# Modulation vectors from row-major weights on VectorE, gate rows built from columns, and an issue order searched from four first ranks

## The chip, the cores and the metric

The kernel runs on one core of one Trainium2 chip. The metric is the device time of one execution in microseconds (us); lower is better. Engines are named as in the profile: PE is TensorE (matmuls; PEld its weight loads), DVE is VectorE, ACT is ScalarE, POOL is GpSimd, SP is the queue that issues every DMA.

## What is computed

A two-layer transformer block with modulation, followed by a third mixer block that the change does not touch. What matters here is the modulation: a vector `c` of 1024 values gives, for each of two layers, 3072 numbers (shift, scale, gate), through a 1024 x 3072 matrix.

```python
cond = jax.nn.silu(c)
for layer in range(DEPTH):                       # DEPTH = 2, D_MODEL = 1024, SEQ = 512
    mod = cond @ w_ada[layer] + b_ada[layer]
    shift, scale, gate = jnp.split(mod, 3, axis=-1)
    h = rmsnorm(x, g_pre[layer]) * (1.0 + scale[:, None, :]) + shift[:, None, :]
    y = even_mixer(h, ...) if layer % 2 == 0 else odd_mixer(h, ...)
    x = x + gate[:, None, :] * rmsnorm(y, g_post[layer])
```

All inputs and the output are float32. The mixers are projections of `h`, several kinds of attention, a gate and an output projection.

## The kernel before

**Modulation.** `w_ada` lies in memory as in the reference: a row per input, 3072 outputs along it. One product of 1024 outputs takes eight transfers of 512 KB (128 inputs on the partitions, 1024 outputs along the row). For each, DVE multiplies the tile by the column `cond[:, k]` and adds it to an accumulator [128, 1024] (`gemv_acc`, L175 for the first, L177 for the other seven). The sum over the 128 partitions is still open then. For shift and scale, `gemv_cols` (L183) closes it with eight PE matmuls against a column of ones, one output column each, and DVE adds the bias (L185): the result is a column tile [128, 8]. For the gate, `gate_row` (L204) closes it with two PE matmuls of ones [128,128] by 512 columns, so that the result stands on all partitions as a row [128, 1024]; bias and `g_post` are broadcast from memory as rows, DVE adds (L216) and POOL multiplies (L217).

**The start.** `first_h` (L645) loads four token blocks `P` of `x`, sums their squares on ACT (L135), scales them (L671), and PE transposes them (L140) into PSUM, from where ACT copies them to `qk` (L677). The scale vector of layer 0 (`pthr` is its accumulator) gives `moda` (L685), with which ACT writes `hh` (L687) and DVE `hl` (L693). Then PE multiplies with the first three weight chunks (`whir` and `wlor` are the two halves of a loaded weight `wrawr`, written by ACT at L109 and POOL or DVE at L113; `accr` is PSUM). The shift vector of layer 0 (`sa`) is summed meanwhile and applied afterwards (L724 to L727).

**The background.** The other four products (scale and shift of layer 1, the two gates) run as background steps through one buffer, `graw`: layer 1's and gate 0 during layer 0, gate 1 during layer 1. The gate row is needed where layer 0 and layer 1 end (`residual`, L606 and following, at about 268 us and 564 us of the profile).

**The order.** What an engine issues next is set by `Plan.pin` (L2043): it reads all instructions, gives each a rank (its place in the program, mixed with the length of the path behind it, weight `PATH`), lists them by a model of durations, ranks them backward from the result, and repeats this six times; the order with the shortest modelled end is fixed for every engine. So a change anywhere moves instructions everywhere.

## Time and profile before

| | |
|---|---|
| median of 3 runs | 960.73 us (960.22 to 961.03) |
| the profiled execution's own time | 959.33 us |
| span of that execution, first to last instruction | 957.6 us |
| PE busy | 908.6 us (95%) |
| DVE busy | 707.7 us (74%) |
| ACT busy | 535.0 us (56%) |
| POOL busy | 243.7 us (25%) |

The profile is of one execution. Its own time is 1.7 us above its span (what lies before the first and behind the last instruction), and 1.4 us below the median of the runs. A busy share is a mean over the span; an engine that is busy is not always the one that the others wait for.

### The profile page before, as it was taken

How to read it: one execution, taken by the hardware profiler on the slowest of the kernel's cores; microseconds unless marked ns; L12 is line 12 of the kernel's file. 1: busy time of each engine (PE TensorE's matmuls, PEld its weight loads, DVE VectorE, ACT ScalarE, POOL GpSimd, SP SyncE). 2: the span in 40 equal slices, each digit the busy share in tenths (PEclk: the TensorE clock that was granted, in tenths of full speed). 3: DMA queues.
4: the chain of work that ended last, by engine and by line, in shares of the span. 5: the costliest groups of instructions: out<-in, count | busy, mean ns of one | idle time of the engine just before them, and what ended most of it. 6: DMA issues, size and time to landing. Idle time of an engine off the chain costs nothing.

```text
span 957.6 us, 14806 instructions
## 1 busy us (share of the span) xinstructions
PE 908.6 (95%) x5001; PEld 764.1 (80%) x5001; DVE 707.7 (74%) x1581; ACT 535.0 (56%) x1182; POOL 243.7 (25%) x274
## 2 busy tenths in 40 slices
PE   0999999889989989999999999999999999999996
PEld 0888888768868878889888878987888888888775
DVE  5876869858989747875465766377598788687857
ACT  5544677648735435584365944464444486676820
POOL 0330133113410012321021420024044335444530
PEclk9999999989999999999999999999999999999998
DMA  9747644456575555631754534234323344430152
GB/s 350 291 134 213 193 134 140 144 159 162 160 238 203 181 166 142 197 103 48 196 147 117 172 110 145 89 111 144 120 67 87 98 110 105 122 110 24 52 168 88
DMA packets 54623, 137.38 MB, mean 143 GB/s; under 512 B 12983, under 2 KB 13383, under 8 KB 54548
## 3 DMA queue, kind: packets, MB, share of 16 engines
q1 hardware_dynamic: 54548, 136.44, 47.3%
q8 instruction: 40, 0.66, 0.3%
q14 instruction: 35, 0.29, 0.1%
HBM read 105.42 MB, written 8.44 MB: 119 GB/s over the span
## 4 chain that ended last, share of the span: by engine, by line
PE 68%; DVE 12%; DMA 11%; ACT 4%; issue 3%; SPq 2%; POOL 0%; DVEq 0%; ACTq 0%; POOLq 0%
PE accr L80 46%; PE sr L80 10%; PE o L80 6%; PE tr L140 4%; DMA qk<-qk 2%; DMA tmpr<-tmpr 2%; DMA wrawr<-in_w_ev_dram 1%; DVE wlor L113 1%; DMA wrawr<-in_w_out_dram 1%; DMA graw<-in_w_ada_dram 1%; DMA ident<-in_ident_dram 1%; DMA og<-in_w_ada_dram 1%; PE sr L140 1%; SPq L370 1%; DMA qk<-tmpr 1%
## 5 line engine op out<-in xcount | busy, mean ns | idle before, releaser
L80 PE MATMUL accr<-hh,whir 128*128 128x512 f32 x516 | 206.9, 402 | 1.6 <-DVE V L95 1.6
L80 PE MATMUL accr<-hl,whir 128*128 128x512 f32 x516 | 206.5, 401 | 0.0
L80 PE MATMUL accr<-hh,wlor 128*128 128x512 f32 x516 | 205.4, 399 | 0.0
L109 ACT CAST whir<-wrawr 128x1024 fp32r<-128x1024 f32 (+4 forms) x110 | 111.3, 1013 | 105.8 <-PE accr L80 65.7
L113 DVE TENSOR_TENSOR wlor<-wrawr,whir 128x1024 fp32r<-128x1024 f32 (+7 forms) x93 | 111.5, 1202 | 69.6 <-ACT whir L109 69.1
L398 POOL TENSOR_SCALAR Pr<-Pr,sm 128x256 f32<-128x256 f32 (+2 forms) x120 | 76.2, 651 | 229.9 <-DVE sm L1157 76.5
L388 ACT ACTIVATE Pr<-Pr,nm 128x256 f32<-128x256 f32 (+3 forms) x176 | 95.8, 547 | 41.2 <-DVE nm L386 40.4
L80 PE MATMUL accr<-whir,hh 128*128 128x256 f32 (+4 forms) x364 | 116.3, 324 | 2.1 <-DVE tmpr L880 0.6
L80 PE MATMUL accr<-wlor,hh 128*128 128x256 f32 (+4 forms) x364 | 115.7, 321 | 0.0
L80 PEld LDWEIGHTS accr<-hh,whir 128*128 128x128 f32 x516 | 98.0, 190 | 21.4 <-issue 2.9
L80 PE MATMUL accr<-whir,hl 128*128 128x256 f32 (+4 forms) x364 | 114.4, 321 | 0.7 <-DVE hl L95 0.7
L80 PEld LDWEIGHTS accr<-hh,wlor 128*128 128x128 f32 x516 | 97.7, 190 | 19.1 <-issue 0.9
L80 PEld LDWEIGHTS accr<-hl,whir 128*128 128x128 f32 x516 | 98.0, 190 | 18.4 <-issue 0.8
L80 PE MATMUL sr<-qk,qk 128*128 128x256 f32 (+11 forms) x400 | 94.8, 335 | 5.4 <-DMA qk<-qk 2.6
L95 DVE TENSOR_TENSOR ptl<-tr,pthr 128x256 fp32r<-128x256 f32 (+3 forms) x160 | 71.0, 464 | 20.9 <-ACT pthr L90 18.2
L80 PEld LDWEIGHTS sr<-qk,qk 128*128 128x128 f32 (+2 forms) x400 | 69.3, 198 | 17.3 <-DMA qk<-qk 3.4
L80 PEld LDWEIGHTS accr<-whir,hh 128*128 128x128 f32 x364 | 68.8, 190 | 8.8 <-PE accr L140 0.9
L80 PEld LDWEIGHTS accr<-whir,hl 128*128 128x128 f32 x364 | 68.4, 189 | 5.5 <-DVE hl L95 0.9
L80 PEld LDWEIGHTS accr<-wlor,hh 128*128 128x128 f32 x364 | 68.8, 190 | 4.0 <-issue 0.2
L140 PE MATMUL tr<-ident,Pr 128*128 128x128 f32 x392 | 68.4, 282 | 1.9 <-DVE ptl L95 1.5
L90 ACT CAST pthr<-tr 128x384 fp32r<-128x384 f32 (+3 forms) x124 | 52.3, 438 | 25.2 <-PE tr L140 24.0
L386 DVE CUSTOM_DVE_ANT_0 Pr<-sr,cm 128x128 f32<-128x128 f32 (+3 forms) x96 | 45.0, 484 | 25.7 <-PE sr L80 25.2
(374 smaller groups left out, 1740.2 us busy)
## 6 DMA issues: line engine op xcount, KB each, us to landing
graw<-in_w_ada_dram SPq DMA_DIRECT2D x32, 512.0 KB
wrawr<-in_w_od_dram SPq DMA_DIRECT2D x30, 512.0 KB
wrawr<-in_w_dram SPq DMA_DIRECT2D x29, 512.0 KB
qk<-qk SPq DMA_DIRECT2D x111, 128.0 KB
wrawr<-in_w_out_dram SPq DMA_DIRECT2D x24, 512.0 KB
wrawr<-in_w_ev_dram SPq DMA_DIRECT2D x17, 512.0 KB
V<-in_w_ada_dram SPq DMA_DIRECT2D x14, 512.0 KB
qk<-tmpr SPq DMA_DIRECT2D x34, 128.0 KB
```

Source lines behind the costliest of these rows:

```text
L80: self.nc.tensor.matmul(out, a, b, start=start, stop=stop, skip_group_check=True)
L90: self.nc.scalar.copy(hi, src)
L95: self.nc.vector.tensor_tensor(lo, src, hi.bitcast(F32), ALU.subtract)
L109: self.nc.scalar.copy(hi[:, :n], raw[:, :n])
L113: eng.tensor_tensor(lo[:, :n], raw[:, :n], hi[:, :n].bitcast(F32), ALU.subtract)
L140: self.nc.tensor.transpose(out, in_, self.ident[:k, :k])
L370: self.nc.sync.dma_start(dst.bitcast(F32), src.bitcast(F32))
L386: nc.vector.tensor_tensor_reduce(out=Pi, in0=ps[:, :N], in1=add(i), op0=ALU.add, op1=ALU.min, scale=-c, scalar=1e38 if init is None else i ...
L388: nc.scalar.activation(Pi, Pi, AF.Exp, bias=nm[:, i:i + 1], scale=-1.0, accum_out=s[:, i:i + 1])
L398: self.nc.gpsimd.tensor_scalar(v, v, r[:, i:i + 1], 1.0, ALU.mult, ALU.mult)
```

## The change

**Weights.** The matrix is laid out on the host with a row per output (`w_ada` transposed per layer). A transfer of 512 KB now holds 128 outputs on the partitions and their 1024 inputs along the row. `cond_row` makes, once, a tile `crow` [128, 1024] that holds `cond` along the row on every partition: eight PE matmuls of a broadcast column of `cond` against the identity, copied from PSUM by ACT (two copies of 512). It stays in the buffer `sa` until the last product. `gemv` then takes one DVE instruction per transfer (`tensor_tensor_reduce`: multiply with `crow`, sum along the row, start from the bias) and the accumulator read that goes with it; it writes one column of the [128, 8] result. `gemv_acc`, `gemv_cols` and their PE matmuls are gone.

**Gate rows.** The gate comes as a column tile as well. Its bias and `g_post` are loaded as columns (`gcol`, 128 x 16), applied by two small DVE instructions, and `spread` turns the column into a row on all partitions: a PE transpose to [8, 128], an ACT copy, a DMA to DRAM and a broadcast DMA back (as was done already for scale and shift of layer 1).

**Start.** The identity, used by `cond_row`, is asked for first in the program.

**Order.** The planner tries four values of `PATH` with six rounds each, and keeps the best of 24 instead of the best of 6. [...]

```diff
-    def gemv_acc(self, acc, raw, k, eng="dve"):
...
-            self.nc.vector.tensor_scalar(acc, raw, c, None, ALU.mult)
-        else:
-            self.nc.vector.scalar_tensor_tensor(acc, raw, c, acc, ALU.mult, ALU.add)
-
-    def gemv_cols(self, acc, bias, n=8):
...
+    def gemv(self, out, raw, layer, c, init=0.0):
+
+        self.nc.sync.dma_start(raw, self.I["w_ada"][layer, c * 128:(c + 1) * 128, :])
+        self.nc.vector.tensor_tensor_reduce(out=raw, in0=raw, in1=self.crow, op0=ALU.mult, op1=ALU.add,
+                                            scale=1.0, scalar=init, accum_out=out)
+
+    def cond_row(self):
+
+        nc = self.nc
+        self.crow = self.t([128, 1024], "sa")
+        for h in range(2):
+            ps = self.p("s")
+            for j in range(4):
+                c = 4 * h + j
+                self.mm(ps[:, j * 128:(j + 1) * 128], self.cond[:, c:c + 1].to_broadcast([128, 128]), self.ident, j == 0, j == 3)
+            nc.scalar.copy(self.crow[:, h * 512:h * 512 + 512], ps)
...
     def gate_row(self):
         nc = self.nc
-        layer, acc = self.gsum
-        rows = self.t([128, 2, 1024], "V")
...
+        layer, col = self.gsum
+        g = self.t([128, 16], "lamx")
+        nc.sync.dma_start(g, self.I["gcol"][layer])
+        nc.vector.tensor_tensor(col, col, g[:, 0:8], ALU.add)
+        nc.vector.scalar_tensor_tensor(col, col, -0.5, g[:, 8:16], ALU.mult, ALU.mult)
+        return self.spread(col, "V")
...
-    PATH, ROUNDS = 0.10, 6
+    PATHS, ROUNDS = (0.06, 0.1, 0.16, 0.25), 6
...
         if kind == "CustomDveAnt":
-            return 155 + 1.04 * n, 150 + 1.04 * n, 0
+            return 155 + 1.04 * n, 150 + 1.04 * n, port
...
+        for w in self.PATHS:
+            rank = [i / n * (1 - w) - w * p / top for i, p in enumerate(path)]
+            for _ in range(self.ROUNDS):
+                tries.append(self.forward(rank))
+                rank = self.backward(tries[-1][1])
```

The order differs at most places; three of them are shown. The first is SP at the program's start, before the change (`Pr` are the token blocks, `lamx` is `c`; `V` and `og` hold `w_ada`, `wrawr` a weight):

```order
L651 DMA Pr_7_82<-in_x_dram 128x1024
L76 DMA lamx_64<-in_c_dram 128x8
L651 DMA Pr_8_84<-in_x_dram 128x1024
L663 DMA V_97<-in_w_ada_dram 128x1024
L651 DMA Pr_9_86<-in_x_dram 128x1024
L663 DMA V_97<-in_w_ada_dram 128x1024
L663 DMA og_102<-in_w_ada_dram 128x1024
L651 DMA Pr_10_88<-in_x_dram 128x1024
L663 DMA og_102<-in_w_ada_dram 128x1024
L663 DMA V_107<-in_w_ada_dram 128x1024 x2
L663 DMA V_112<-in_w_ada_dram 128x1024 x2
L107 DMA wrawr_61_259<-in_w_ev_dram 128x1024
```

After the change the queue begins with block, block, `c`, block, identity, block, and behind these stand (`bada` and `gpre` are bias and norm weights as columns):

```order
L164 DMA V_111<-in_w_ada_dram 128x1024
L76 DMA bada_107<-in_bada_dram 128x32
L164 DMA V_111<-in_w_ada_dram 128x1024
L107 DMA wrawr_62_260<-in_w_ev_dram 128x1024
L164 DMA V_121<-in_w_ada_dram 128x1024
L164 DMA og_116<-in_w_ada_dram 128x1024
L107 DMA wrawr_69_301<-in_w_ev_dram 128x1024
L164 DMA og_116<-in_w_ada_dram 128x1024
L164 DMA V_126<-in_w_ada_dram 128x1024
L164 DMA V_121<-in_w_ada_dram 128x1024
L76 DMA gpre_105<-in_gpre_dram 128x16
L164 DMA V_126<-in_w_ada_dram 128x1024
```

The token blocks moved in front of the modulation weights, and two weight chunks (`wrawr`) moved in between them; the first product's last transfer is the 14th of 512 KB now and was the 12th.

The second place is DVE where the scale vector of layer 0 is finished. Before, the last sums into `pthr` are followed by three of the next product, the bias (`modc`) and the scale (`moda`):

```order
L177 SCALAR_TENSOR_TENSOR pthr_14_96<-V_112,cond_72,pthr_14_96 128x1024
L175 TENSOR_SCALAR sa_258<-V_265,cond_72 128x1024
L177 SCALAR_TENSOR_TENSOR sa_258<-V_265,cond_72,sa_258 128x1024
L185 TENSOR_TENSOR modc_226<-o_225,bada_94 128x4
L177 SCALAR_TENSOR_TENSOR sa_258<-V_270,cond_72,sa_258 128x1024
L685 SCALAR_TENSOR_TENSOR moda_237<-modc_226,gpre_92 128x4
```

After, `ISA` with 128x1024 is the new sum and `ISA` with 128x1 its accumulator read; `sa_84` is `crow`:

```order
L165 ISA og_116,modc_109<-og_116,sa_84,bada_107 128x1024
L165 ISA modc_109 128x1
L165 ISA V_126,modc_109<-V_126,sa_84,bada_107 128x1024
L165 ISA modc_109 128x1
L669 SCALAR_TENSOR_TENSOR moda_239<-modc_109,gpre_105 128x4
L165 ISA V_121,modc_109<-V_121,sa_84,bada_107 128x1024
L165 ISA modc_109 128x1
L677 SCALAR_TENSOR_TENSOR hl_241<-qk_188,moda_239,hh_240 128x512
```

The first half of the scale now stands directly behind the sixth of its eight sums, with no PE step and no sum of another product between.

The third place is SP where layer 0 passes from its windowed to its latent attention (the copies `qk<-qk` open the latter; `graw` are background transfers). Before:

```order
L157 DMA graw_2088<-in_w_ada_dram 128x1024
L76 DMA cst_3341<-in_ut_dram 128x512
L209 DMA V_2825<-in_b_gate_dram 128x1024
L210 DMA V_2825<-in_g_post_dram 128x1024
L107 DMA wrawr_629_2845<-in_w_out_dram 128x1024
L157 DMA graw_2171<-in_w_ada_dram 128x1024
L157 DMA graw_2230<-in_w_ada_dram 128x1024
L107 DMA wrawr_636_2883<-in_w_out_dram 128x1024
L370 DMA qk_2056<-qk_2052 64x512
```

After, from behind the first transfer of gate 0 to the first copy:

```order
L1015 DMA sink_3306<-in_od_fb_dram 128x8
L107 DMA wrawr_522_2427<-in_w_mla_dram 128x640
L164 DMA graw_2138<-in_w_ada_dram 128x1024
L76 DMA subln_3303<-in_od_subln_dram 128x1
L164 DMA graw_2197<-in_w_ada_dram 128x1024
L76 DMA cst_3308<-in_ut_dram 128x512
L107 DMA wrawr_625_2812<-in_w_out_dram 128x1024
L164 DMA graw_2316<-in_w_ada_dram 128x1024
L164 DMA graw_2388<-in_w_ada_dram 128x1024
L107 DMA wrawr_632_2850<-in_w_out_dram 128x1024
L164 DMA graw_2507<-in_w_ada_dram 128x1024
L355 DMA qk_2034<-qk_2030 64x512
```

Three transfers of gate 0 stood in front of that copy before the change; now it is six, one above the piece and five in it; the two row loads of gate bias and `g_post` are gone.

## Rows read from the trace of the kernel before

**Rows 1.** The page, its first part: busy us and share of span.

```profile
PE 908.6 (95%) x5001; PEld 764.1 (80%) x5001; DVE 707.7 (74%) x1581; ACT 535.0 (56%) x1182; POOL 243.7 (25%) x274
```

**Rows 2.** Who PE waited for: us, times, longest.

```profile
PE sr L140 <- DMA ident<-in_ident_dram: 21.8, 1, 21.8
PE accr L80 <- DVE V L606: 2.6, 1, 2.6
```

**Rows 3.** Stretches: length, busy us by engine, PE clock, DMA share, GB/s.

```profile
22.00:32.00 10.00, 10.00 (x49) 10.00 (x49) 8.70 (x7) 6.37 (x11) 5.32 (x2) 1.00 1.03 408
...
220.00:240.00 20.00, 19.61 (x125) 16.52 (x124) 19.45 (x61) 19.01 (x55) 6.39 (x10) 1.00 0.58 158
```

**Rows 4.** Timeline of the start: start us, us, engine, line.

```profile
4.35 1.06 ACT L135 ACTIVATE tmpr<-Pr 128x1024 bf16<-128x1024 f32 x1 [2.27 <-DMA Pr<-in_x_dram]
...
20.37 1.15 ACT L671 ACTIVATE Pr<-Pr,st_r 128x1024 f32<-128x1024 f32 x1 [3.17 <-DVE st_r L129]
21.45 1.04 ACT L109 CAST whir<-wrawr 128x1024 fp32r<-128x1024 f32 x1
...
21.76 0.87 PE L140 MATMUL sr<-ident,Pr 128*128 128x128 f32 x3 [21.76 <-DMA ident<-in_ident_dram]
...
26.26 2.97 POOL L113 TENSOR_TENSOR wlor<-wrawr,whir 128x1024 fp32r<-128x1024 f32 x1 [1.34 <-ACT whir L109]
...
27.06 3.26 DVE L177 SCALAR_TENSOR_TENSOR sa<-V,cond,sa 128x1024 f32<-128x1024 f32 x1
...
28.64 0.59 ACT L677 COPY qk<-tr 128x512 f32<-128x512 f32 x1 [0.27 <-PE tr L140]
...
29.04 1.71 PE L80 MATMUL o<-ones,pthr 128*128 128x1 f32 x8
...
30.48 2.56 ACT L687 ACTIVATE hh<-qk,moda 128x512 fp32r<-128x512 f32 x4 [1.25 <-DVE moda L685]
...
31.57 1.20 PE L80 MATMUL accr<-hh,whir 128*128 128x512 f32 x2
```

**Rows 5.** Timeline of PE around the modulation matmuls, at two places.

```profile
45.65 0.95 PE L80 MATMUL o<-ones,sa 128*128 128x1 f32 x8
46.46 0.49 PE L80 MATMUL accr<-hh,wlor 128*128 128x512 f32 x1
...
561.93 0.39 PE L80 MATMUL accr<-whir,qk 128*128 128x512 f32 x1
562.16 1.02 PE L80 MATMUL o<-sa,ones 128*128 128x512 f32 x2
...
563.25 0.39 PE L80 MATMUL accr<-wlor,qk 128*128 128x512 f32 x1
```

**Rows 6.** DVE and PE groups, shapes apart: busy us, mean ns; last, one line's minimum, median, maximum.

```profile
L177 DVE SCALAR_TENSOR_TENSOR sa<-graw,cond,sa 128x1024 f32<-128x1024 f32 x28 | 36.9, 1317 | 4.5 <-DMA graw<-in_w_ada_dram 4.5
L386 DVE CUSTOM_DVE_ANT_0 Pr<-sr,cm 128x512 f32<-128x512 f32 x24 | 16.4, 683 | 1.4 <-PE sr L80 1.3
L386 DVE DVE_READ_ACCUMULATOR2_ANT nm<- 128x1 f32 x176 | 14.5, 82 | 0.0
...
L140 PE MATMUL o<-ident,modc 128*8 128x128 f32 x1 | 0.3, 272 | 0.0
...
L1024 DVE CUSTOM_DVE_ANT_0 tmpr<-tmpr x2: 220/220/221, 312.7 to 315.4; 128x64 f32<-128x64 f32 x2
```

**Rows 7.** Timeline where the latent attention starts.

```profile
188.90 0.33 SPq L157 DMA_DIRECT2D graw<-in_w_ada_dram  x1
...
194.78 1.28 DVE L177 SCALAR_TENSOR_TENSOR sa<-graw,cond,sa 128x1024 f32<-128x1024 f32 x1 [2.01 <-DMA graw<-in_w_ada_dram]
...
197.58 2.84 SPq L370 DMA_DIRECT2D qk<-qk  x4
...
199.81 1.28 DVE L177 SCALAR_TENSOR_TENSOR sa<-graw,cond,sa 128x1024 f32<-128x1024 f32 x1 [0.34 <-DMA graw<-in_w_ada_dram]
...
207.25 0.47 PE L80 MATMUL sr<-qk,qk 96*128 96x128 f32 x2 [1.65 <-DMA qk<-hh]
```

More of the change, by code (lines that the diff above doesn't have):

```diff
@@ L152, in sigmoid @@
         nc.vector.tensor_tensor(out, out, b, ALU.mult)
-    def wada(self, layer, k, c0):
-        raw = self.t([128, 1024], "graw")
-        self.nc.sync.dma_start(raw, self.I["w_ada"][layer, k * 128:(k + 1) * 128, c0:c0 + 1024])
-        return raw
     GE = 'dve'
@@ L165 @@
     KF = 2
-    def gemv_acc(self, acc, raw, k, eng="dve"):
-        c = self.cond[:, k:k + 1]
-        if eng == "pool":
-            dst = acc if k == 0 else raw
-            self.nc.gpsimd.tensor_scalar(dst, raw, c, 1.0, ALU.mult, ALU.mult)
-            if k:
-                self.nc.gpsimd.tensor_tensor(acc, acc, raw, ALU.add)
-        elif k == 0:
-            self.nc.vector.tensor_scalar(acc, raw, c, None, ALU.mult)
-        else:
-            self.nc.vector.scalar_tensor_tensor(acc, raw, c, acc, ALU.mult, ALU.add)
-    def gemv_cols(self, acc, bias, n=8):
-        ps = self.p("o")
-        out = self.t([128, 8], "modc", 6)
-        for j in range(8):
-            self.mm(ps[:, j:j + 1], acc[:, j * 128:(j + 1) * 128], self.ones[:, 0:1], j == 0, j == 7)
-            if j % n == n - 1:
-                self.nc.vector.tensor_tensor(out[:, j + 1 - n:j + 1], ps[:, j + 1 - n:j + 1], bias[:, j + 1 - n:j + 1], ALU.add)
-        return out
+    def gemv(self, out, raw, layer, c, init=0.0):
[11 more added lines that the diff above has]
+            nc.scalar.copy(self.crow[:, h * 512:h * 512 + 512], ps)
     def gemv_steps(self, layer, parts, done):
         for part in parts:
-            acc = self.t([128, 1024], "sa")
+            col = self.t([128, 8], "modc", 6)
             for k in range(8):
-                self.gemv_acc(acc, self.wada(layer, k, part * 1024), k, self.GE)
+                b = 16 * layer + 8 * part + k
+                self.gemv(col[:, k:k + 1], self.t([128, 1024], "graw"), layer, 8 * part + k, self.bada[:, b:b + 1] if part < 2 else 0.0)
                 yield
-            done(part, acc)
+            done(part, col)
     def bg(self, n=1):
@@ L205, in gate_row @@
         nc = self.nc
-        layer, acc = self.gsum
-        rows = self.t([128, 2, 1024], "V")
-        row, g = rows[:, 0], rows[:, 1]
-        nc.sync.dma_start(row, self.I["b_gate"][layer:layer + 1, :].to_broadcast([128, 1024]))
-        nc.sync.dma_start(g, self.I["g_post"][layer:layer + 1, :].to_broadcast([128, 1024]))
-        nc.gpsimd.tensor_scalar(g, g, -0.5, 1.0, ALU.mult, ALU.mult)
-        for h in range(2):
-            s = slice(h * 512, h * 512 + 512)
-            ps = self.p("o")
-            self.mm(ps, self.ones, acc[:, s], True, True)
-            nc.vector.tensor_tensor(row[:, s], ps, row[:, s], ALU.add)
-        nc.gpsimd.tensor_tensor(row, row, g, ALU.mult)
-        return row
+        layer, col = self.gsum
[4 more added lines that the diff above has]
+        return self.spread(col, "V")
     def mod_a(self, layer, scale):
@@ L256, in spread @@
         self.tr(ps[0:8, 0:128], col)
-        row = self.t([128, 1024], "pth")
+        row = self.t([128, 1024], tag)
         self.nc.scalar.copy(row[0:8, 0:128], ps[0:8, 0:128])
@@ L656, in first_h, with steps @@
         pair = {}
-        def steps(part, acc, ks):
+        def steps(part, col, ks):
             for k in ks:
@@ L661, in steps @@
                     pair[part] = self.t([128, 2, 1024], "og" if (part, k) == (1, 2) else "V")
-                raw = pair[part][:, k % 2]
-                nc.sync.dma_start(raw, self.I["w_ada"][0, k * 128:(k + 1) * 128, part * 1024:(part + 1) * 1024])
-                self.gemv_acc(acc, raw, k)
-        acc1 = self.t([128, 1024], "pth")
-        steps(1, acc1, range(8))
+                b = 8 * part + k
+                self.gemv(col[:, k:k + 1], pair[part][:, k % 2], 0, b, self.bada[:, b:b + 1])
+        sc, sh = (self.t([128, 8], "modc", 6) for _ in range(2))
+        steps(1, sc, range(8))
         xT = []
@@ L727, in first_h, with mod_done @@
             eng.tensor_tensor(lo, x, hi.bitcast(F32), ALU.subtract)
-    def mod_done(self, part, acc):
-        self.modv[part] = self.gemv_cols(acc, self.bada[:, 16 + 8 * part:24 + 8 * part])
+    def mod_done(self, part, col):
+        self.modv[part] = col
     def even(self):
```

19 lines of the change are left out of this document (6 added, 13 removed).

## The prediction

> **What bounds the kernel now.** I read four views in this order. The page's first part says which engine the time belongs to: PE is busy in 95% of the span, the next engine, DVE, in 74% [rows 1]. The list of waits says what PE's idle time is: 957.6 - 908.6 = 49 us are idle, 21.8 of them one wait at the very start, and the longest of the others is 2.6 us [rows 2]. So behind the start PE hardly waits, and work taken off PE is worth about its own time. The stretches say where that is less safe: from 220 to 240 us PE has 19.61 and DVE 19.45 busy us of 20, both full, so there DVE must not get more work [rows 3]. The timeline of the start shows how the first 31.57 us come about: the fourth token block is scaled at 20.37, PE's first transpose comes at 21.76, the modulation matmuls sit among the transposes, and the first `hh` waits at 30.48 for the scale `moda`; the first projection matmul follows at 31.57 [rows 4]. The chain behind `moda` is: transfers, DVE sums, PE matmuls, DVE. DVE's own step in it came late, since a sum of the next product begun at 27.06 took 3.26 us, most of it beside a POOL instruction that ran from 26.26 for 2.97 us [rows 4].
>
> **Matmuls removed and added.** 32 one-column matmuls and 4 gate matmuls go; 8 for `crow` and 2 transposes come.
> - Four one-column matmuls (eight records) hold PE from 45.65 to 46.46, 0.81 us, or 0.20 each [rows 5]. 24 of them lie behind the start: 4.9 us.
> - A gate matmul: from 561.93 to 563.25 PE does two ordinary matmuls, which start 0.23 us apart (561.93 to 562.16), and one gate matmul: 1.32 - 0.46 = 0.86 us [rows 5]. Four: 3.4 us.
> - The added transposes: the same form took 0.27 us [rows 6], its start to the next start less; two cost at most 0.5, I take 0.4.
> - The other eight one-column matmuls and the eight for `crow` belong to the start.
>
> Behind the start PE loses 4.9 + 3.4 - 0.4 = 7.9 us of work. Eight of the matmuls (1.6 us) stood shortly before the stretch in which PE waits for the copies that open the latent attention [rows 7]; there a shorter PE only waits longer. I count 6.3.
>
> **DVE.** A sum was 1317 ns on average in the background [rows 6]. The new instruction is of a form that the trace has, on other shapes: 683 ns for 512 elements with one input in PSUM, 220 ns for 64 with both in SBUF [rows 6]. That is (683 - 220) / 448 = 1.03 ns an element, and 683 + 512 x 1.03 = 1212 ns for 1024; with the accumulator read of 82 ns, 1.30 us. For 32 background sums that is no more than before. The bound from below is 1.21 (the read hidden); from above 3.26, the longest that a sum of this size took, beside POOL [rows 4]. I take 1.30, since the two rows of the form lie on one line. The DVE additions to bias and gate rows go, a few small ones come; nothing for either, since DVE waits for PE elsewhere, and where it does not, they are fewer.
>
> [...]
>
> **The start after the change.** A transfer of 512 KB at 408 GB/s takes 1.28 us [rows 3]. Before, the 13th such transfer was there by 21.45, when ACT began to cast it [rows 4]. Counted from that, in the new order of SP the fourth token block (4th) is there at 21.45 - 9 x 1.28 = 9.9, the first modulation tile (5th) at 11.2, the two weight chunks (7th, 10th) at 13.8 and 17.6, the tile of the sixth sum (12th) at 20.2.
> - `crow`: ACT squares the fourth block (1.06 us and a read-out, until about 11.2), copies half of `crow` (0.59), scales a block (1.15), copies the other half (0.59) [rows 4]: complete at 13.5. PE's eight matmuls for it, at the start's pace of 1.71 us for four [rows 4], lie before that, while PE had nothing to do.
> - DVE: six sums of 1.30 from 13.5 would end at 21.3; the sixth tile makes it 20.2 + 1.3 = 21.5. Behind the first sum, which waits for `crow`, stand DVE's small steps for the third and fourth block, for which ACT waits: at most 1.3 us, and ACT has a cast to do meanwhile.
> - ACT: behind 13.5 stand small roots (some 0.6, an estimate), three more scales (3.4), two casts (2.1) and eight copies (4.7): 24.3, with some waits for transposes 25.
> - POOL: its first two instructions now fall among the sums. Each could hold DVE by up to 2.97 us, as at 27.06 [rows 4]; then the half scale comes at 21.5 + 5.9 = 27.4.
>
> So the first `hh` comes between 25 and 27.4 and the first projection matmul 1.1 later, at 26.1 to 28.5 instead of 31.57: 3.1 to 5.5 us. I take 4.5. Below that, up to nothing, if the late `crow` (the first sum needs all of it) and POOL add up; above it 6, if `c` and the casts come early. Cover for the shift vector: its eight sums run while PE does 72 projection matmuls at 0.23, 16.6 us; its last tile ends the first 28 times 512 KB of SP's new order, 21.45 + 15 x 1.28 = 40.7, its last sum ends at 42, and PE would need the shift at 27 + 16.6 = 43.6. If that cover is gone, each microsecond counts.
>
> **The gate row by DRAM.** The new path (DVE, PE, ACT, DMA out, DMA in) replaces PE, DVE and POOL. For gate 1 all sums are done far ahead. For gate 0, PE waited 2.6 us for what uses the row [rows 2]; the new path is longer but its last sum stands further ahead. I count the wait as unchanged; bounds: it vanishes (2.6 gained) or doubles.
>
> **SP where the latent attention starts.** Here an added wait is likely. The buffer `graw` is one, so each transfer stands in SP's queue until the sum of the one before is done, and all that is behind it waits, the copies `qk<-qk` too. The cycle was 188.90 to 194.78 + 1.28, 7.2 us, and the next about 5.0 (196.1 to 199.81 + 1.28) [rows 7]. Before, one such cycle lay between 188.90 and the copy at 197.58. Now, with gate 0's first three sums done by then, two do: the copy comes at 189.4 + 2 x 5.0 = 199.4, or with 7.2, at 203.8. That is 1.8 to 6.2 us later, and PE waited for these copies already (1.65 us at 207.25) [rows 7]. The slower cycle had the two row loads beside it that are gone now, so I take 1.8.
>
> **The order.** All engines' orders are new, chosen from 24 and not 6. No row prices that. Since PE waited 27 us behind the start, it cannot give more than that; I take nothing, with 3 us either way.
>
> **Sum.** 4.5 (start) + 6.3 (PE) - 1.8 (SP) = 9.0 us. The profiled execution took 959.33, 957.6 within its span, so 950.3 for one like it; its median stands 1.4 higher: 951.7, rounded to 951.5.
>
> **Rivals.**
> - *Nothing gained at the start* (0.15): `crow` and POOL delay the scale to 30. For it: DVE's 3.26 us. Against: two thirds of the old path (PE steps of 1.71 us and DVE's late step) are gone. 951.5 + 4.5 = 956.
> - *More gained* (0.17): the copies come no later, PE's waits shrink with the new order. 951.5 - 1.8 - 1.6 - 3 = 945.
> - *SP's queue decides* (0.06; slower): all of the cycles behind gate 0's first sum, five, take 7.2 us, so the copies come after 209 instead of 197.58, and PE waits 11.5 us longer at 207. It decides from a delay of 11 us on, when start and PE's work (10.8) are eaten. 960.7 - 10.8 + 11.5 = 961.5, and more if the delay is longer. Against: the row loads are gone.
> [...]
> - My forecast: 0.58, by itself 947 to 955.5.
>
> **Range and chances.** Forecast, nothing gained and most of "more gained" make 943 to 958.5, which leaves out the two slow cases and the tails. About 0.2% (2 us) is what a measurement of this kernel can tell from no change: 958.8 and 962.6 are the bounds. Faster: 0.57 + 0.13 + 0.17 = 0.87. Within: 0.05, from the edges of the forecast, of nothing gained and of SP's queue. Slower: 0.08.
>
> **What would show it.** Right, if in the new profile: the first projection matmul starts at 26 to 28.5; the new sum takes 1.2 us, and its group has about 48 of them; PE's busy time falls by some 8 us behind the start; the wait for `qk<-hh` at the latent attention is 1.5 to 4 us. Wrong, if the first projection starts at 30 or later (start), if sums take over 2 us (DVE), if PE's waits behind the start sum to over 35 us instead of 27 (order, SP), or if `accr` waits long for `V` at the end of layer 0 (gate row).

## The result, and the profile after

The changed kernel takes 974.52 us (median of 4 runs, 972.83 to 982.74), the kernel before beside it 960.48 (4 runs, 959.6 to 961.03): a ratio of 1.0164, 95% interval 1.0138 to 1.0191. It is 1.6% slower; 951.5 was forecast, with 943 to 958.5 as the range. The profiled execution is the one of 982.74, some 8 us above the others, and its mean granted clock is the lowest of the four (0.969; the others 0.974 to 0.978). So sizes below are read from its trace with that in mind.

The page's first part and PE's waits (who waited for what: us, times, longest), which answer to [rows 1] and [rows 2]:

```profile
PE 918.4 (94%) x4947; PEld 762.8 (78%) x4947; DVE 704.8 (72%) x1623; ACT 537.4 (55%) x1186; POOL 238.2 (24%) x270
```

```profile
PE sr L80 <- DVE st_r L129: 8.5, 1, 8.5
PE accr L80 <- DVE V L591: 4.6, 1, 4.6
PE sr L80 <- DMA qk<-hh: 3.9, 3, 2.0
PE accr L80 <- ACT hh L671: 3.2, 1, 3.2
...
```

PE is idle for 981.0 - 918.4 = 62.6 us instead of 49.0, though its long wait at the start fell from 21.8 us to 8.5 (the first row). And it is busy for longer (918.4 instead of 908.6) with less to do. What makes it so is the granted clock: 0.969 over the span instead of 0.987. In the changed kernel the matmuls of 128 rows and 512 columns (the wide ones) start 0.23 us apart from 656.97 to 661, at a clock of 1.00, and 0.43 us apart from 673 to 677, at 0.50 (half clock, from here on). So (1 - clock) x span is about what the clock costs, an estimate: 30.4 us after, 12.4 before. The mean doesn't count the slow pace of PE's first matmuls in the kernel before: its transposes start 0.21 us apart from 22.43 on, and its wide matmuls 0.43 and not 0.23 until 34.27. By that pace it is some 6 us of work in 12, an estimate (so the 1.00 that [rows 3] has for 22 to 32 is not what PE ran at). So the 23.4 us between the two spans are 13.6 us more of idle time, 12 to 18 more of half clock, and 2 to 8 less of work.

Stretches tell where. Columns: length, busy us of PE, PEld, DVE, ACT, POOL, PE's granted clock, DMA share, GB/s. After, then before:

```profile
0.00:32.00 32.00, 17.03 (x67) 13.57 (x68) 20.36 (x50) 22.93 (x42) 6.44 (x8) 0.84 0.97 362
160.00:240.00 80.00, 65.56 (x351) 51.90 (x350) 61.20 (x171) 53.13 (x136) 16.36 (x24) 0.94 0.51 139
640.00:900.00 260.00, 253.46 (x1450) 210.33 (x1449) 191.60 (x454) 141.44 (x298) 98.44 (x122) 0.96 0.34 96
```

```profile
160.00:240.00 80.00, 72.87 (x405) 60.85 (x404) 64.31 (x177) 55.41 (x142) 17.56 (x28) 0.91 0.53 150
640.00:900.00 260.00, 258.01 (x1544) 215.29 (x1543) 206.58 (x508) 154.66 (x331) 103.37 (x132) 1.00 0.34 95
```

In the first 32 us PE now does 17.03 us of work instead of 10.24 before. From 160 to 240 it is idle for 14.4 us instead of 7.1. From 640 to 900, where the change has no instruction of its own, it loses 4.5 us more, and the clock falls from 1.00 to 0.96, another 10 us. Behind 32 us PE is idle for 62.6 - 15.0 = 47.6 us; before 49.0 - 21.8 = 27.2. The prediction had named 35 us of such waits as a sign that it is wrong.

The start did what was forecast (timeline, to be read beside [rows 4]):

```profile
12.39 0.58 ACT L177 COPY sa<-sr 128x512 f32<-128x512 f32 x1
13.00 1.28 DVE L165 CUSTOM_DVE_ANT_0 V<-V,sa,bada 128x1024 f32<-128x1024 f32 x1 [1.92 <-ACT sa L177]
15.63 2.60 POOL L113 TENSOR_TENSOR wlor<-wrawr,whir 128x1024 fp32r<-128x1024 f32 x1 [14.41 <-ACT whir L109]
15.99 3.32 DVE L165 CUSTOM_DVE_ANT_0 V<-V,sa,bada 128x1024 f32<-128x1024 f32 x1
...
24.96 0.15 DVE L669 SCALAR_TENSOR_TENSOR moda<-modc,gpre 128x4 f32<-128x4 f32 x1
...
25.98 1.22 PE L80 MATMUL accr<-hh,whir 128*128 128x512 f32 x2 [3.23 <-ACT hh L671]
```

`crow` is complete at 12.97, the first sum starts at 13.00. Two of the sums ran beside a POOL instruction (15.63 to 18.23, 18.65 to 21.53) and took 3.32 and 3.37 us instead of 1.28, as feared. The first projection matmul starts at 25.98 instead of 31.57.

And the sums cost what was forecast (groups by shape: busy us, mean ns of one, idle before them; the first two of five):

```profile
L165 DVE CUSTOM_DVE_ANT_0 graw<-graw,sa,bada 128x1024 f32<-128x1024 f32 x16 | 20.6, 1290 | 1.5 <-DMA graw<-in_w_ada_dram 1.4
L165 DVE CUSTOM_DVE_ANT_0 graw<-graw,sa 128x1024 f32<-128x1024 f32 x16 | 19.9, 1242 | 1.5 <-DMA graw<-in_w_ada_dram 1.3
...
```

### The profile page after: what moved, and what is told of

Same layout as the page of the kernel before. It is cut to its first block, busy times and chain, and to the rows that moved or that the text cites. A ratio compares the mean times of both kernels' runs of the same rounds, so it can differ in the third digit from the quotient of the medians.

```text
span 981.0 us, 14747 instructions
## 1 busy us (share of the span) xinstructions
PE 918.4 (94%) x4947; PEld 762.8 (78%) x4947; DVE 704.8 (72%) x1623; ACT 537.4 (55%) x1186; POOL 238.2 (24%) x270
## 5 line engine op out<-in xcount | busy, mean ns | idle before, releaser
L80 PE MATMUL accr<-hh,whir 128*128 128x512 f32 x516 | 206.7, 405 | 5.4 <-ACT hh L671 3.2
L80 PE MATMUL accr<-hl,whir 128*128 128x512 f32 x516 | 207.4, 405 | 1.7 <-DVE hl L677 1.7
L80 PE MATMUL accr<-hh,wlor 128*128 128x512 f32 x516 | 207.7, 405 | 0.0
L80 PEld LDWEIGHTS accr<-hh,whir 128*128 128x128 f32 x516 | 98.4, 191 | 28.1 <-ACT hh L671 3.6
L80 PE MATMUL accr<-whir,hh 128*128 128x256 f32 (+4 forms) x364 | 115.8, 326 | 1.5 <-DVE hl L95 1.0
L80 PE MATMUL accr<-whir,hl 128*128 128x256 f32 (+4 forms) x364 | 115.5, 325 | 0.7 <-DVE hl L95 0.7
L80 PE MATMUL accr<-wlor,hh 128*128 128x256 f32 (+4 forms) x364 | 115.3, 323 | 0.0
L80 PEld LDWEIGHTS accr<-hl,whir 128*128 128x128 f32 x516 | 98.8, 191 | 20.9 <-DVE hl L677 2.6
L80 PEld LDWEIGHTS accr<-hh,wlor 128*128 128x128 f32 x516 | 98.5, 191 | 19.8 <-issue 1.8
L80 PE MATMUL sr<-qk,qk 128*128 128x256 f32 (+11 forms) x400 | 97.0, 334 | 12.9 <-DMA qk<-hh 3.9
L80 PEld LDWEIGHTS sr<-qk,qk 128*128 128x128 f32 (+2 forms) x400 | 67.7, 194 | 27.0 <-DVE nm L371 5.7
L140 PE MATMUL tr<-ident,Pr 128*128 128x128 f32 x392 | 72.6, 283 | 4.2 <-DVE ptl L95 2.6
L80 PEld LDWEIGHTS accr<-whir,hh 128*128 128x128 f32 x364 | 69.1, 192 | 8.2 <-DVE hl L95 1.2
L80 PEld LDWEIGHTS accr<-whir,hl 128*128 128x128 f32 x364 | 69.2, 191 | 5.8 <-DVE hl L95 0.9
L80 PEld LDWEIGHTS accr<-wlor,hh 128*128 128x128 f32 x364 | 69.3, 192 | 3.9
L371 DVE CUSTOM_DVE_ANT_0 Pr<-sr,cm 128x128 f32<-128x128 f32 (+2 forms) x96 | 45.4, 484 | 30.3 <-PE sr L80 29.5
```

The costliest lines, as they stand in the source:

```text
L80: self.nc.tensor.matmul(out, a, b, start=start, stop=stop, skip_group_check=True)
L140: self.nc.tensor.transpose(out, in_, self.ident[:k, :k])
L371: nc.vector.tensor_tensor_reduce(out=Pi, in0=ps[:, :N], in1=add(i), op0=ALU.add, op1=ALU.min, scale=-c, scalar=1e38 if init is None else i ...
```

## The experiments

**Is it the work or its order?** The first four kernels part the two. The first is the change with the planner of before, the second the change with its four ranks and only `port` out of the cost of the new sum, the third the kernel before with the planner of the change, the fourth the change with another single rank. `port` is a flag of the planner's model, which plans a DVE instruction that has it behind a POOL instruction that has it, and not beside it, and the other way round; the planner of the change sets it for the sum where both inputs are in SBUF.

```diff
 (first)
-    PATHS, ROUNDS = (0.06, 0.1, 0.16, 0.25), 6
+    PATHS, ROUNDS = (0.1,), 6
-            return 155 + 1.04 * n, 150 + 1.04 * n, port
+            return 155 + 1.04 * n, 150 + 1.04 * n, 0
 (second: the last two lines alone; third: all four the other way, in the kernel before; fourth)
-    PATHS, ROUNDS = (0.06, 0.1, 0.16, 0.25), 6
+    PATHS, ROUNDS = (0.06,), 6
```

> [...] All the changed work stays. Theory 'search' (the order that the search over four ranks picked leaves PE many small gaps, and the granted clock falls after them): 951 to 958, below the kernel before, since the start gain (5.6 us, first projection at 25.98) and the removed PE work (6 to 8 us) come through. Rival 'work' (sums, their transfers in SP's queue and the gate row by DRAM delay PE in any order): 970 to 976, as the change. Rival 'any new order' (the order of before happened to be a good one, each newly planned one costs 5 to 20 us): 960 to 980, without a relation to the search.

> [...] Theory 'search': the four ranks are still there, 965 to 976. Rival 'port cost' (it is the port in the planner's cost that pushes sums and POOL work to bad places): 950 to 960. Rival 'work': 970 to 976. Rival 'any new order': somewhere from 955 to 980.

> The kernel before with the planner of the change (four first ranks, the port in the cost), none of the changed work. Theory 'search': slower than before, 968 to 978. Rival 'work': as before, 957 to 963. Rival 'any new order': 960 to 980.

> The changed kernel with one first rank of weight 0.06 and the port cost: another order of the same work. Theory 'search' does not fix it. Rival 'work': 970 to 976, as the change. Rival 'any new order': off the other orders by several us either way, 955 to 980, with the share of half clock going with the time.

| Kernel | us (runs) | ratio to before, interval |
|---|---|---|
| change, planner of before | 964.75 (7) | 1.0058, 1.0034 to 1.0081 |
| change, no `port` in the cost | 965.48 (4) | 1.0073, 1.0053 to 1.0093 |
| kernel before, planner of the change | 977.36 (4) | 1.0204, 1.018 to 1.0227 |
| change, rank 0.06 | 971.66 (4) | 1.014, 1.0097 to 1.0183 |

The first lies between what the first two theories gave, in the range of the third. The first two kernels turned out to be one and the same program: without `port` in the cost, the search over four ranks picks the order that the old rank gives. With it, the search picks the third round of rank 0.16. That pick costs the changed kernel 974.52 against some 965. The third run is the clearest: not one of the changed instructions is in it, and the new planner alone (it picks rank 0.16 there too) makes the kernel before 18 us slower. It fits the search theory, and 'any new order' (960 to 980) as well. What the planner of these kernels computes says why it took these orders: its modelled end is 913.1 us for the pick of the change and 924.2 for the best of rank 0.10 at the same costs, and 918.7 against 919.3 for the work of before. So on the work of before the search gained 0.6 us in the model and lost 18 on the chip. The order is the main cause of the loss. It isn't the whole: in the old planner's order the work by itself ought to have gained, and it lost 0.6%.

**Where the order of the change costs.** At two places of the second block. At the first, PE gets its narrow work in one lump (timeline of the changed kernel; stretches of 10 us below it):

```profile
661.79 0.48 PE L80 MATMUL accr<-hh,wlor 128*128 128x512 f32 x1
662.21 0.93 PE L80 MATMUL sr<-tmpr,tmpr 64*128 64x128 f32 x6
...
668.25 2.07 PE L80 MATMUL sr<-sa,tmpr 128*128 128x128 f32 x8
...
672.48 0.79 PE L80 MATMUL accr<-hh,whir 128*128 128x512 f32 x1
673.07 0.63 PE L80 MATMUL accr<-hl,whir 128*128 128x512 f32 x1
673.50 0.63 PE L80 MATMUL accr<-hh,wlor 128*128 128x512 f32 x1
```

```profile
660.00:670.00 10.00, 10.00 (x48) 6.38 (x47) 5.12 (x14) 6.74 (x8) 0.74 (x1) 0.89 0.16 54
670.00:680.00 10.00, 10.00 (x34) 6.78 (x34) 5.53 (x11) 1.26 (x2) 4.18 (x6) 0.60 0.43 126
...
860.00:870.00 10.00, 8.59 (x33) 6.83 (x32) 4.80 (x15) 3.35 (x10) 1.62 (x3) 0.61 0.05 16
870.00:880.00 10.00, 10.00 (x54) 8.23 (x53) 7.30 (x23) 6.11 (x15) 4.12 (x4) 0.87 0.18 47
```

Between 661.79 and 672.48 there is no matmul of 128 rows and 512 columns. PE has no gap (10.00 of 10), yet the granted clock falls to 0.89 and then 0.60, and the wide matmuls from 672.48 on start 0.43 us apart instead of 0.23 (0.50 from 673 to 677). The kernel before has 1.00 in both stretches. The second place is at 860, behind a wait for a DMA and with matmuls of 32 columns:

```profile
861.78 0.28 PE L80 MATMUL accr<-kch,qk 128*128 128x32 f32 x1 [1.41 <-DMA qk<-tmpr]
```

By (1 - clock) x length each place costs some 5 us in this execution, an estimate. The kernel before with the new planner, which has none of the changed work and an order of rank 0.16 too, has both:

```profile
660.00:670.00 10.00, 10.00 (x45) 5.74 (x44) 5.55 (x15) 6.74 (x8) 0.32 (x1) 0.77 0.17 56
670.00:680.00 10.00, 10.00 (x38) 7.01 (x37) 6.15 (x14) 1.26 (x2) 5.30 (x8) 0.71 0.53 145
...
860.00:870.00 10.00, 10.00 (x45) 8.62 (x44) 6.54 (x22) 3.73 (x10) 1.71 (x3) 0.66 0.00 0
```

A later run settles what this half costs: the change in its own order up to the end of the first of the two blocks, and from there in the order of the run with the old planner.

```diff
-        start = min(tries)[1]
+        start = ranks   # a table: the order of the change up to 580 us as the planner counts, then the other
```

> The changed kernel in its own order up to the end of the first block of the reference's two (about 590 us), and from there in the order of the run with the old planner. No work differs. Theory 'order' (the second half of the changed order bunches narrow matmuls from 661 to 672 us and has more waits at 810 to 862; half clock follows both): 962 to 966, some 10 us less than the change. Rival 'the loss is made in the first half, where the changed work is': 972 to 976.

965.1 us (11 runs), ratio 1.0048 (1.0027 to 1.0068). The same work, the second half in another order: 9.4 us back by the medians, 1.2% by the ratios, as the order theory had it. In 640 to 900 PE is as busy as before, at a clock of 1.00:

```profile
640.00:900.00 260.00, 258.81 (x1540) 215.60 (x1538) 204.41 (x500) 152.12 (x328) 103.05 (x131) 1.00 0.35 97
```

**How much do orders of the work of before differ?** Five rounds of the old planner instead of six, and rank 0.06 instead of 0.10, in the kernel before:

> The kernel before with five rounds of the planner instead of six, so that it takes another order of the same work from the same first rank. Theory 'order': nearby orders differ by several us, so 960 to 975, with more PE gaps and half clock where it is slower. Rival 'orders from one first rank are alike': 957 to 962.

> The kernel before with a first rank of weight 0.06 instead of 0.10. Theory 'order' (the order of before is a good one among those that the planner makes): 963 to 980. Rival 'the order of before is like the others': 955 to 963.

961.57 us (10 runs; 1.0021, 1.0 to 1.0043) and 975.29 (4 runs; 1.0149, 1.0116 to 1.0183). The first is within the range of either theory, the second is what the order theory gave. The order of before is at the good end of a spread of 18 us, and a near one is nearly as good. One more order of the changed work, rank 0.10 with `port` left in the cost:

> The changed kernel with one first rank of weight 0.10 as before, but with the port in the cost of the new sum: one more order of the same work, between the run with the old planner (964.75) and the change (974.5). Theory 'order' (any order differs by several us from the next): 962 to 978, with PE's idle time and half clock going with it. Rival 'it is the weight 0.16 that is bad': 963 to 967.

962.86 (10 runs; 1.0024, 1.0 to 1.0048), at the low end of what the order theory gave. Its rival's 963 to 967 begins 0.14 us above it, so this run doesn't part the two. Taken together, the planner's orders fall in two groups by their first rank, whichever work they hold: rank 0.10 gives 960 to 965 us (960.2, 961.6; 964.8, 962.9), ranks 0.06 and 0.16 give 972 to 977 (975.3, 977.4; 971.7, 974.5). Eight orders are few, and an order close to one of rank 0.10 can be as bad (972.6, further below).

With rank 0.10 the changed work is 0.2 to 0.6% slower than the kernel before, with rank 0.06 some 0.1% and with rank 0.16 some 0.4% faster than the work of before at the same rank (1.014 / 1.0149 and 1.0164 / 1.0204). The two orders of each pair differ as well, so this is no clean price of the work; but in none of the pairs is it worth the 9 us of the forecast.

**What PE's work is worth.** Two runs change PE's work alone, in exactly the order of before: one does each of the 16 one-column matmuls of layer 1 four times (the sums are then four times too large), the other leaves out 20 of the 24 one-column matmuls behind the start (the modulation is then not the reference's).

```diff
 (more)
-            self.mm(ps[:, j:j + 1], acc[:, j * 128:(j + 1) * 128], self.ones[:, 0:1], j == 0, j == 7)
+            for q in range(4):
+                self.mm(ps[:, j:j + 1], acc[:, j * 128:(j + 1) * 128], self.ones[:, 0:1], ...)
 (fewer)
+            if j % n == 0:
+                self.mm(ps[:, j:j + n], acc[:, j * 128:(j + 1) * 128], self.ones[:, 0:n], ...)
```

> The kernel before in exactly its order, where each of the 16 one-column matmuls of layer 1's modulation is done four times: 48 more, at 0.20 us each 9.7 us more PE work, about 125 and 180 us. Only the price of PE work is tried; the values summed are four times too large. If PE's work behind the start is worth its own time, as the prediction took it: 968 to 971. If other engines or transfers set the time there: 960 to 964.

> The kernel before in exactly its order, where 20 of the 24 one-column matmuls behind the start are left out (one matmul makes the four or eight columns of its group from the first 128 rows' sums, so the modulation is not the reference's). 20 x 0.20 us = 4.0 us of PE work less. If PE's work behind the start is worth its time: 954.5 to 957.5. If waits take its place: 958.5 to 961.

More: 982.24 us (5 runs), ratio 1.0235 (1.0211 to 1.0258), 22 us for 9.7 us of work, above the range of either theory. Fewer: 960.77 (12 runs), ratio 1.0004 (0.9986 to 1.0021), nothing for 4 us of work, as the second theory had it; the 0.9958 that it would be worth lies outside the interval. Of the run with more, stretches, a timeline row and the page row; then the page row of the run with fewer:

```profile
130.00:140.00 10.00, 10.00 (x62) 9.57 (x60) 5.04 (x9) 3.30 (x7) 3.73 (x4) 0.75 0.42 120
140.00:150.00 10.00, 10.00 (x45) 9.29 (x45) 2.70 (x9) 2.05 (x7) 0.00 (x0) 0.56 0.16 52
200.00:210.00 10.00, 10.00 (x64) 10.00 (x64) 3.08 (x6) 1.77 (x4) 1.04 (x1) 0.67 0.55 185
```

```profile
132.44 11.22 PE L82 MATMUL o<-ones,sa 128*128 128x1 f32 x64
```

```profile
PE 930.6 (95%) x5097; PEld 784.8 (80%) x5097; DVE 708.6 (72%) x1581; ACT 535.4 (54%) x1182; POOL 246.8 (25%) x274
```

```profile
PE 904.0 (94%) x4961; PEld 756.9 (79%) x4961; DVE 706.8 (74%) x1581; ACT 535.2 (56%) x1182; POOL 247.0 (26%) x274
```

With fewer, PE is busy 4.6 us less and idle 958.5 - 904.0 = 54.5 us instead of 49.0, in the two profiled executions: the time became waiting. With more, PE has no gap from 130 to 150, but the granted clock falls while the 32 one-column matmuls (64 records) run from 132.44 to 143.6, so that the stretches have 0.75 and 0.56, and it falls again behind 200 (0.67). The work is paid once, and by the same estimate the half clock costs more than that again: (1 - 0.973) x 983.1 = 26.5 us against 12.4.

**The waits that took its place.** In the run with the old planner PE's two largest waits behind the start were these:

```profile
PE accr L80 <- DVE V L591: 5.2, 1, 5.2
PE accr L80 <- DVE qk L315: 3.8, 1, 3.8
```

```profile
202.26 1.23 DVE L165 CUSTOM_DVE_ANT_0 graw<-graw,sa 128x1024 f32<-128x1024 f32 x1 [4.65 <-DMA graw<-in_w_ada_dram]
203.41 0.69 DVE L315 TENSOR_TENSOR qk<-accr,qk 128x512 fp32r<-128x512 f32 x1
204.15 0.50 PE L80 MATMUL accr<-hh,whir 128*128 128x512 f32 x1 [3.80 <-DVE qk L315]
```

The first is the gate row by DRAM. The second is a sum that stood in DVE's queue for its 512 KB, 4.65 us, with PE's next eviction (`qk`) behind it. I tried each by itself and both together, in the order of that run: a second buffer for `graw`, whose transfers were to go out one step earlier, and gate rows made by PE (a broadcast gate column times the identity) and copied by ACT. With an instruction more or less the planner, placing by the ranks of that run, moved a few dozen of its other PE instructions. (Kernels with a table of ranks have two lines more at their head, so L82 is L80 of the change; the gate row by PE adds seven.)

```diff
-                self.gemv(col[:, k:k + 1], self.t([128, 1024], "graw"), ...)
+                self.gemv(col[:, k:k + 1], self.t([128, 1024], "graw", 2), ...)
 (gate row)
-        return self.spread(col, "V")
+        row = self.t([128, 1024], "V")
+        for h in range(2):
+            ps = self.p("o")
+            for j in range(4):
+                c = 4 * h + j
+                self.mm(ps[:, j * 128:(j + 1) * 128], col[:, c:c + 1].to_broadcast([128, 128]), self.ident, j == 0, j == 3)
+            nc.scalar.copy(row[:, h * 512:h * 512 + 512], ps)
+        return row
```

> The changed kernel in the order of the run with the old planner (964.75), with a second buffer for the background tiles of w_ada, so that each transfer is issued one step earlier. Theory 'late transfers' (a sum stands in DVE's queue for its transfer and holds what PE waits for: DVE 4.65 us at 202.26, PE 3.80 at 204.15, then half clock for 3.4 us): that wait goes, 958 to 961. Rival 'other causes': PE's wait at 204 only shifts, 963 to 967.

> The changed kernel in the order of the run with the old planner (964.75), and the gate rows made by PE and ACT instead of by DRAM. Theory 'gate row' (PE waited 5.16 us for V at 281.96, then half clock for 6.8 us, which is another 3.4): less 8.6 at most, plus some 3 for the added matmuls, 958 to 961. Rival 'other causes': 963 to 967.

> Both of these edits together in that order. If the two waits are what the order of the old planner lost against the kernel before: 952 to 957, below before. If the waits only move: 960 to 967.

972.61 us (1.0133, 1.0106 to 1.0159), 968.97 (1.0111, 1.0085 to 1.0137) and 969.43 (1.0096, 1.0073 to 1.0119), 6 runs each: all three slower than the 964.75 that they set out from, and above the ranges of both theories. But the first and the third have no second buffer. The kernel's table of buffers goes before the number in the call:

```python
    BUFS = {..., 'graw': 1, ...}
    def t(self, shape, tag, bufs=1, dt=F32):
        bufs = self.BUFS.get(tag, bufs)
```

So `graw` stayed one buffer, as in the run with the old planner, where a transfer goes out when the sum before it is done: one is issued at 195.03, behind a sum from 193.78 to 195.00. These two runs change the order alone, and the first says what that can cost: the same work in an order close to that of the old planner's run takes 7.9 us more. What a second buffer would give is not shown. The second run has its edit; with the gate row by PE its wait is gone, and a new one of 2.1 us stands behind it (the 3.8 us for `qk` are those of L315 above, nine lines further down here):

```profile
PE accr L82 <- DVE qk L324: 3.8, 1, 3.8
...
PE sr L142 <- DVE st_r L129: 2.1, 1, 2.1
```

```profile
290.00:300.00 10.00, 9.38 (x45) 7.53 (x44) 9.96 (x26) 4.98 (x15) 0.00 (x0) 1.00 0.73 235
300.00:310.00 10.00, 7.88 (x63) 7.47 (x61) 9.96 (x21) 4.00 (x12) 0.86 (x1) 1.00 0.66 213
310.00:320.00 10.00, 9.56 (x54) 8.82 (x52) 8.28 (x24) 3.91 (x10) 0.08 (x1) 0.66 0.15 59
```

From 290 to 310 DVE is full (9.96 of 10) and PE idles 2.7 us, and from 310 the clock falls to 0.66. So a part of what the gate row gave back is lost there. (In the change the clock is 0.50 from 280 to 284, behind the wait of 4.60 us for the gate row; in the run with the old planner its mean from 240 to 420 is 0.96.) The profile is of the fastest of the six executions (964.34); why the median is 4.6 us above it is not shown. Before these I had tried both forms of the gate row in the order of the kernel before, as far as the planner could keep it by its ranks:

> All of the changed work, issued in the order of the kernel before as far as it goes: each instruction that both kernels have gets as its rank the start that the planner gave it before, each new sum that of the sum it replaces, and the planner places in one pass by these ranks. Theory 'order' (the change lost by its new order; the work by itself gains at the start and on PE): 948 to 955. Rival 'work' (in any order the sums, their transfers or the gate row by DRAM cost more than the start and PE's removed matmuls give): 960 to 970. If the gate row alone is at fault, PE waits 5 us or more for V at the end of layer 0 and the time is 953 to 958.

> As the run in the order of before, and the gate row is made by PE (eight matmuls of a broadcast gate column with the identity and two ACT copies for each of the two rows) instead of a trip through DRAM. Theory 'order': the gate row is a small part of it, 2 to 4 us less than in the run before it where PE waited about 5 us for V at the end of layer 0, while PE gets some 3 us of matmuls more. Rival 'gate row': 5 us or more less, and the wait for V falls to 2 us or less.

982.57 (6 runs) and 976.42 (6 runs). These don't show what the work is worth in that order. The bias `bada` kept its late place in SP's queue, where the sums of before didn't need it and the new ones do, so the first sum came at 22.67, and PE waited 19.8 us for `hh` at the start and 9.0 us for `V` at the end of layer 0. Between the two the 9.0 us wait for the gate row makes 6 us, as the rival 'gate row' had it, in this bad order.

**Does a gain at the start reach the end?** Small matmuls of ones, which nobody reads, keep PE busy in its waits at the start: 21 in the changed work in exactly the order of the run with the old planner, 12 in the kernel before in exactly its own.

```diff
 (change, behind each group of transposes)
+            for _ in range(7 if c == 7 else 2):
+                self.mm(warm[:, 0:128], self.ones, self.ones, True, True)
 (before, ahead of the first transpose)
+        for _ in range(12):
+            self.mm(warm[:, 0:128], self.ones, x0[1][:, 0:128], True, True)
```

> The changed kernel in exactly the order of the run with the old planner (964.75), with 21 small matmuls of ones that nobody reads, put between the transposes of the start, where PE waits. They change nothing that is computed. In that order PE ran its first projections at half clock from 24.1 to 34.3. Theory 'half clock' (the early start is half eaten by it): the projections run at full clock from 25 or so, 4 to 5 us less, 959 to 962. Rival 'the chain behind is the limit': time as without them, 963 to 967; and if they stand in the way of the transposes, up to 969.

> The kernel before in exactly its order, with 12 small matmuls of ones that nobody reads, ahead of the first transpose, in PE's wait of 21.76 us. Before, PE ran at half clock from there to about 34 (0.43 us from one transpose pair or projection matmul to the next instead of 0.23). Theory 'half clock': the matmuls from 21.76 on run at full clock, PE's part of the chain to the first projection shrinks by 2 to 3 us and the first 2.7 us of projections by half: 954 to 958. Rival 'the chain behind is the limit': 958 to 961.

967.97 (6 runs; 1.0087, 1.0061 to 1.0113) and 959.49 (12 runs; 0.9987, 0.9963 to 1.0011): no gain in either, as the rival had it. But in neither did the projections start earlier: in the profiled executions the first one comes at 24.72 instead of 23.21 in the first run and at 32.77 instead of 31.57 in the second. So what an earlier start is worth at the end, neither shows. In the second the transposes did run at twice the pace, 0.11 us apart instead of 0.21, and PE then waited 3.29 us for DVE, where a sum took 3.20 us (the 3.26 of [rows 4], in the same order, were beside POOL):

```profile
23.20 0.27 PE L142 MATMUL tr<-ident,Pr 128*128 128x128 f32 x1
26.75 3.20 DVE L179 SCALAR_TENSOR_TENSOR sa<-V,cond,sa 128x1024 f32<-128x1024 f32 x1 [0.18 <-DMA V<-in_w_ada_dram]
30.08 1.87 PE L82 MATMUL o<-ones,pthr 128*128 128x1 f32 x8 [3.29 <-DVE modc L187]
```

In the first, the added matmuls stood in front of the projections, and behind a wait of 1.03 us at 28.38 PE fell to the slow pace again (wide matmuls 0.43 us apart from 30.73 on). Its first 32 us hold 18.00 us of work at clock 0.95, against 16.96 at 0.82 without, but that counts the matmuls that nobody reads.

**A version slightly ahead of before.** The run with the old planner stood some 3 to 4 us ahead of before at 180 us (by the matmul columns that PE had done), and the one with rank 0.10 and `port` lost little from there on. So I took the first order up to there and the second behind it, with no change in the work (the table of ranks again, cut at about 180 us).

> The changed kernel in the order of the run with the old planner up to about 180 us (there it stood 4 us ahead of the kernel before) and from there in the order of the run with rank 0.10 and port (which from there on kept pace with the kernel before). Theory 'order': 955 to 959, faster than before. Rival 'a gain does not outlive the next wait' (as with the start kept busy): 961 to 966.

958.86 us (12 runs, beside 960.24 for before), ratio 0.9976, 0.996 to 0.9992: at the upper end of what the order theory gave. It is the only one of these kernels whose whole interval is below 1, by 0.24%. It was put together with the traces in hand, and two near orders of before differ by as much (1.0021), so this 0.24% can't be put down to the changed work. Page row and stretches:

```profile
PE 905.1 (95%) x4947; PEld 755.7 (79%) x4947; DVE 703.7 (74%) x1623; ACT 535.6 (56%) x1186; POOL 239.3 (25%) x270
```

```profile
160.00:240.00 80.00, 69.44 (x393) 56.87 (x392) 65.79 (x186) 55.40 (x145) 18.45 (x28) 0.96 0.49 136
```

## Why the prediction was wrong

The accounts of the profiled executions (idle is span less PE's busy time; half clock is (1 - mean clock) x span, the estimate from above). The mean clock of the kernel before went from 0.984 to 0.993 over 28 executions, so the last column has the mean of that over all runs that were taken (their number in brackets; for before, those beside the last three experiments):

| Kernel | span | PE busy | idle | half clock | half clock, all runs |
|---|---|---|---|---|---|
| before | 957.6 | 908.6 | 49.0 | 12.4 | 11.3 (28) |
| the change | 981.0 | 918.4 | 62.6 | 30.4 | 25.6 (4) |
| change, planner of before | 963.0 | 906.5 | 56.5 | 17.3 | 19.4 (7) |
| kernel before, planner of the change | 975.4 | 913.9 | 61.5 | 20.5 | 19.5 (4) |
| before, fewer one-column matmuls | 958.5 | 904.0 | 54.5 | 8.6 | 12.7 (12) |
| two orders | 957.1 | 905.1 | 52.0 | 17.2 | 18.1 (12) |

- **The order** is the step that failed: "Since PE waited 27 us behind the start, it cannot give more than that; I take nothing, with 3 us either way." The bound was drawn on the side of the gain alone; the new order made waits that weren't there, and half clock with them (61.5 and 20.5 us instead of 49.0 and 12.4, for the work of before). Measured: 18 us for the new planner without the changed work; and in the changed kernel over 9 us for the order of the second block alone, where the prediction had looked for nothing. None of its slower rivals had an order in it.
- **PE's removed work** (6.3 us) failed too, on its premise that "work taken off PE is worth about its own time" because PE hardly waits. The work did go; in the order of before 4 us of it were worth nothing. PE's busy share of 95% didn't make it the limit at each of its hand-overs. Between 170 and 320 us PE's waits are for DVE, ACT and transfers in turn; that a chain through all of them sets the time there is argued from these waits, not tried. What the runs show is that PE's idle time took what PE gave.
- **The start** (4.5) was right in its mechanism and, at 25.98 us, 0.12 us better than the range for the first projection. It didn't reach the end. The first matmul behind the gate row of layer 0, the same in all three kernels, starts at 276.99 before, at 280.62 in the change and at 281.96 in the run with the old planner: by then the lead of the start is gone and 3.6 to 5.0 us more are lost (before, the change, the old planner):

```profile
276.99 0.79 PE L80 MATMUL accr<-whir,qk 128*128 128x512 f32 x1 [2.56 <-DVE V L606]
```

```profile
280.62 0.80 PE L80 MATMUL accr<-whir,qk 128*128 128x512 f32 x1 [4.60 <-DVE V L591]
```

```profile
281.96 0.79 PE L80 MATMUL accr<-whir,qk 128*128 128x512 f32 x1 [5.16 <-DVE V L591]
```

- **The sum** was right: 1242 and 1290 ns on average for the 32 in the background, and 79 ns for the readout, so some 1.3 us together; there are 48 in all. The sum of before took 1317 ns [rows 6]. Over 2 us, the prediction's sign that it is wrong here, are two of the 48, those beside POOL. Of its "two slow cases" one is SP's queue; the other would be sums that are slow throughout, and no run shows it: the means are these.
- **The gate row**, counted as unchanged, came out at its upper bound of 5.2 and beyond: 4.6 us of waiting for `V` in the change, 5.2 with the old planner, 5.6 in the two orders, instead of 2.6.
- **SP at the latent attention** (-1.8): the first copy was issued at 197.68 instead of 197.58 in the changed order, and PE's waits for `qk<-hh` were 3.9 us in three, within the 1.5 to 4 that was given. So this slow rival was not the cause.

That waits and half clock took the gain is shown by the accounts and by the runs with PE's work changed. Why one order loses more than another is shown for the second block, at the two places at 661 and 860 us. The first block costs the change's own order nothing against that of the old planner: with the second block exchanged it takes 965.1, beside 964.75. What both lose there against the kernel before, from 160 to 420 us, stays open wait by wait: the one that I took away, for the gate row, was followed by another, and the one for `graw` was not taken away. Whether the changed work or its order loses these last 0.2 to 0.6% is not shown.

## What to carry to other kernels

When a change lets a planner order everything anew, price the order first, by giving the new planner the old work and the old planner the new work; here that was worth more than every term of the work together. A search over more orders is only as good as the model that picks: here the model had the better order 11 us behind the worse one. Work taken off the busiest engine need not be worth its time: here 4 us less on PE gave 960.77 us beside 960.24, with 54.5 us of idle time instead of 49.0. The same edit in an unchanged order tells. Add to the account of idle time what the granted clock takes: here it fell to 0.60 behind narrow matmuls in a row (670 to 680 us of the change), where PE had no idle time at all.

## What the runs showed of the hardware

- The granted clock fell without any gap on PE (10.00 of 10 in each stretch): while 64 one-column matmul records ran in a row for 11.22 us from 132.44 in the run with more of them (stretches at 0.75 and 0.56), and in the changed kernel among narrow matmuls between the wide ones at 661.79 and 672.48 (0.89 and 0.60). In the changed kernel the wide matmuls behind them started 0.43 us apart instead of 0.23, until 677.77.
- Adding one-column matmuls to PE cost 22 us for 9.7 of work (ratio 1.0235) and removing some gave nothing for 4 (1.0004): the price of a microsecond of PE was not the same in the two directions.
- A two-input DVE sum of 1024 elements beside a POOL tensor_tensor took 3.26 to 3.37 us instead of 1.28, the old form (3.26 in [rows 4]) as the new one (3.32, 3.37).
